# Expert inputs gathered by indirect DMA from normed rows in HBM, instead of by 0/1 products on TensorE

## The chip, the cores and the metric

The kernel runs on one core of a Trainium2 chip. The metric is the device time of one execution in microseconds (us), from runs on the chip; lower is better.

## The reference, cut to what matters

Two blocks are computed in float32 at width 1024. The second has two layers (`DEPTH = 2`) of attention followed by a mixture of experts, and the change lies in the latter. Layer 0 routes 512 tokens (256 latent, 256 context), layer 1 only the 256 latent ones. Each token goes to 2 of 32 experts, each with 512 hidden units:

```python
hf = _modulate(_rmsnorm(x, g_ffn[i]), sh_f, sc_f)      # h * (1 + scale) + shift
...
def _hier_moe(h, ...):          # group by argmax, then top 2 of its 8 experts
    ...
    xb = h_pad[tok_buf].reshape(n_blocks, MOE_BLOCK, d)
    y = (silu(xb @ w_gate[e]) * (xb @ w_up[e])) @ w_down[e]
    out = segment_sum(y * w_buf[:, None], tok_buf)
```

So there are 1024 choices of an expert in layer 0 and 512 in layer 1. Every expert has three matrices of 2 MB, 201 MB for a layer. Latent and context tokens have their own gain (norm weight times 1 + scale) and shift for each of the 1024 features.

## The kernel before, in words

The work is written once, in Python, and laid out for five engines that run side by side and wait on each other by semaphores. TensorE is PE, VectorE is DVE, ScalarE is ACT, GpSimd is POOL, SyncE is SP. A scheduler places the instructions; inside `with self.pinned()` PE keeps the order in which the code has them.

**Before a mixture (`attention`, from L1367).** While the attention's output product runs, `after(m)` transposes each 128 features of the residual into token rows and stores them: one copy (`tok`, L1390), and in layer 0 a second with the rounding rest (`low`, L1394), because these rows are later the operand of products in the fast float32r format. `moe` (L1670) then takes each token's 1/rms, `route` (L1493) picks the experts and gives `pos` (for each token and expert its slot, or 0) and `wt` (its weight and its 1/rms, as a high and a low part).

**A pair of experts.** The 32 experts are done as 16 pairs of 64 + 64 slots (128 columns). For pair p the loop in `moe` has, on PE in this order: `up(...,0)`, the gate product (`pgu`, 32 matmuls); `slots(p)` (`pst`), which turns the 0/1 selection `sel` and reads each slot's weight off; `add` of the pair before for features 0 to 3 (`psy`); `up(...,1)` (again `pgu`); `add` 4 and 5; `hidden` (silu, product, four transposes `phe`); then `gather` for pairs to come, if one is due; `add` 6 and 7; `down` (`pdn`, 32 matmuls). `add` brings the result back to the tokens by a product with the turned selection `selT` and DVE adds it to the residual `xT` (L1906). An expert with more than 64 tokens is finished in `overflow`, a loop with a count read at run time, which stands ahead of the pairs.

**The gather (L1761).** `chosen` compares `pos` with 1 to 64 (`sel`, 0 or 1). `gather` multiplies the token rows by `sel`: for each of the 8 feature blocks `pxe` in PSUM, over two halves of the tokens, in layer 0 over latent and context and over copy and rest. `pin` multiplies a row of rms values by `sel`, ACT makes shift times that row (L1799), DVE adds context's share (L1805) and gain times `pxe` (L1807). So `xe` holds h times rms, and `hidden` multiplies by 1/rms. In layer 0 one `gather` serves two pairs (256 columns); in layer 1 it serves one. The first is taken apart and its pieces lie between the first gate product's matmuls.

**The weights.** `Ahead` streams the expert weights, 192 pieces of 1 MB a layer, over the SP queue, in order, into a ring of buffers. A piece is loaded once its buffer's earlier piece has been used. The ring has 15 buffers in layer 0 (L1955: `h0`, `h1`, four of `base`, `b0`, `b1`, `b4`, `b5`, and five of `more_room`) and 20 in layer 1. Up to 14 (18) of them are filled ahead of the routing.

PSUM has eight banks: four in pool `pm` for the large products, four in `pt` for `pst`, `psy`, `phe`, `pin` and `pxe`. `selT` has a single buffer.

Of the kernel before, what the change touches and what calls it, by code (L numbers as in the profile page):

```python
# [22 lines left out]
BIG = 12582912.0  # L23

# [68 lines left out]
class Net:  # L93
# [7 lines left out]
    def setup(self):  # L101
# [7 lines left out]
        self.mod = self.pool("mod", 1)  # L109
        self.cols = c.tile([P, NCOL], F32, name="cols")  # L110
# [1115 lines left out]
    def attention(self, l, x, xT, norm, mods, ex, wx):  # L1226
# [141 lines left out]
        with self.dense(), self.tc.tile_pool(reuse_waits="tile", name="ao", bufs=1) as sc:  # L1368
            self.table(AF.Abs_reciprocal_sqrt)

            toks = [(("b2", "x"), ("b3", "xc")), (("b2",),)][l]
            toks = [[self.place(n, [P, 2, D], F32R if len(z) == 2 else F32, "tok") for n in z] for z in toks]
# [5 lines left out]
            def after(m):  # L1378
# [7 lines left out]

                at = lambda z: z.rearrange("p t (k m a) -> p t m a k", k=8, m=8)[:, :, m]
                pv = ps.rearrange("p u (a k) -> p u a k", k=8)
                for r in range(nx):
                    nc.scalar.activation(at(toks[r][0]), pv[:, 2 * r:2 * r + 2], AF.Copy)  # L1390
                def low():
                    for r, z in enumerate(toks):
                        if len(z) == 2:
                            nc.vector.tensor_tensor(at(z[1]), pv[:, 2 * r:2 * r + 2], at(z[0]), op=ALU.subtract)  # L1394
                if m < KD - 1:
                    low()
                k0 = {3: 0, 6: 4, 7: 7}.get(m)
                if k0 is None:
                    return low
# [9 lines left out]
                return low  # L1409
# [18 lines left out]
            self.low = after(KD - 1)  # L1428
# [10 lines left out]
    def moe_consts(self):  # L1439
# [8 lines left out]
        self.onesr = self.ones.bitcast(F32R)  # L1448

# [15 lines left out]
    def by_rows(self, l, mods, nx, sc):  # L1465
# [10 lines left out]
        nc.vector.tensor_copy(self.rows, ps)  # L1476

# [15 lines left out]
    def route(self, lg, rs, nt, keep, sc):  # L1493
# [70 lines left out]
    def overflow(self, l, m, pos, wt, rs, more, tot, nt, keep, mw, ex):  # L1564
# [6 lines left out]
        with self.tc.For_i(0, n):  # L1571
            with ExitStack() as st:
# [20 lines left out]
                eq = mw.tile([P, 32], F32, name="eq", tag="selT")  # L1593
# [12 lines left out]
                nc.vector.tensor_copy(wx[:, :, 2:4], bc(rs[:, :, None], [P, nt, 2]))  # L1606
# [17 lines left out]
                xe, steps = self.gather(m, sel, mw)  # L1624
                for f in steps:
                    f()
                g = self.up(xe, w, one, 0)
                selT, ws = self.slots(sel, (wh, wl), one, mw)
                add = self.down(m, self.hidden(g, self.up(xe, w, one, 1), ws, mw), selT, ws, w, one, mw)
# [40 lines left out]
    def moe(self, l, toks, xT, ss, lg, mods, ex, room, then):  # L1670
# [6 lines left out]
        with ExitStack() as st:  # L1677
# [4 lines left out]
            rs = keep.tile([P, nt], F32, name="rs")  # L1682
            std = keep.tile([P, 2, nt], F32R, name="std")
            m = (xT, toks, cols, mgain, std)
            with ExitStack() as s2:
# [8 lines left out]
                nc.gpsimd.tensor_copy(rs, r)  # L1694
                nc.gpsimd.tensor_scalar(st1, st1, 1.0 / D, EPS, op0=ALU.mult, op1=ALU.add)
                nc.gpsimd.tensor_tensor(st1, st1, r, op=ALU.mult)
                nc.gpsimd.tensor_copy(std[:, 0], st1)
                nc.gpsimd.tensor_tensor(std[:, 1], st1, std[:, 0], op=ALU.subtract)
                pos, wt, more, tot = self.route(lg, rs, nt, keep, sc)
# [3 lines left out]
            self.overflow(l, m, pos, wt, rs, more, tot, nt, keep, sc, ex)  # L1703
            ex.load(total - len(ex.tiles))
            groups = [slice(0, 64), slice(64, 128)]

            per = 2 * nx
            sel = self.chosen(pos, 0, per, nt, sc)
            xe, steps = self.gather(m, sel, sc, True)

            def first(k):
                for f in steps[:2] if k == 0 else steps[k + 1:k + 2]:
                    f()
            add = None
            for p in range(16):
                Z = slice(128 * (2 * p % per // 2), 128 * (2 * p % per // 2) + 128)
                new = 2 * (p + 1) % per == 0 and p < 15
                ex.until(2 * p + 1)
                w = lambda a, j, k: ex.take(2 * p + a, j, k)
                xz = [v[:, Z] for v in xe]  # L1720
                with self.pinned():
                    g = self.up(xz, w, groups, 0, None, None if p else first)
                    selT, ws = self.slots(sel[:, :, Z], [z[:, :, p] for z in wt], groups, sc)

                    if add:
                        add([0, 1, 2, 3])
                    u = self.up(xz, w, groups, 1)
                    if new:
                        sel = self.chosen(pos, 2 * (p + 1) // per, per, nt, sc)
                    if add:  # L1730
                        add([4, 5])
                    if new and add:
                        add([6, 7])
                    hT = self.hidden(g, u, ws, sc)
                    if p == 15:
                        self.table(AF.Abs_reciprocal_sqrt)
                    if new:
                        xe, steps = self.gather(m, sel, sc)
                        for f in steps:
                            f()  # L1740
                    elif add:
                        add([6, 7])
                    add = self.down(m, hT, selT, ws, w, groups, sc)
# [17 lines left out]
    def gather(self, m, sel, sc, first=False):  # L1761

        nc = self.nc
        toks, std = m[1], m[4]
        nx = len(toks)
        n = sel.shape[2]
        per = 1 if first else 512 // n

        if n == P:
            xe = sc.tile([P, KD, n], F32, name="xe", tag="xe0")  # L1770
            xe = [xe[:, k] for k in range(KD)]
        else:
            xe = [sc.tile([P, 4, n], F32, name="xe", tag=f"xe{i}") for i in range(2)]
            xe = [xe[k // 4][:, k % 4] for k in range(KD)]
        row = sc.tile([P, nx, n], F32, name="row", tag="row")

        def step(k0):
            got = []
            if k0 == 0:

                ps = self.pt.tile([P, nx, n], F32, name="pin", tag="t")
                for u in range(2 * nx):
                    for i in range(2):
                        self.mm(ps[:, u // 2], bc(std[:, i, u:u + 1], [P, P]), sel[:, u], u % 2 == 0 and i == 0, u % 2 == 1 and i == 1)
                nc.scalar.activation(row, ps, AF.Copy)
            for r in range(nx):
                ps = self.pt.tile([P, per, n], F32, name="pxe", tag="t")
                for j in range(per):
                    K = slice((k0 + j) * P, (k0 + j) * P + P)
                    parts = len(toks[r])  # L1790
                    for i, z in enumerate(toks[r]):
                        for t in range(2):
                            s = sel[:, 2 * r + t]
# [220 lines left out]
def bc(ap, shape):  # L2014
    return ap.to_broadcast(shape)
# [58 lines left out]
```

## Time and profile before

| what | value |
|---|---|
| time, median of 3 runs | 2374.86 us (2373.95 to 2375.71) |
| the profiled execution's own time | 2374.64 us |
| its span, first to last instruction | 2372.9 us |
| granted PE clock, mean over the span | 0.980 |
| PE busy / DVE / ACT / POOL | 94% / 55% / 39% / 6% |
| DMA, mean over the span | 261 GB/s |
| expert weights | 384 pieces of 1 MB |

The span lies 1.74 us below the execution's own time. PE is busy for most of the span, but its matmuls are pipelined, so busy time says little of how near it is to its limit. DMA varies from stage to stage, from 89 GB/s in one fortieth of the span to 420 GB/s in others.

### The profile page before, as it was taken

Reading aid. Unit: us, or ns where it says so; the run is one execution under the profiler, and the core shown is the slowest. Engines: PE = TensorE matmul, PEld = TensorE weight load, DVE = VectorE, ACT = ScalarE, POOL = GpSimd, SP = SyncE. Lnnn points to the kernel's source line nnn. Section 1 sums busy time; section 2 is a strip of 40 time slices with the busy share of each in tenths; the row PEclk is TensorE's granted clock in tenths of the full one; section 3 lists DMA queues with packets and bytes.
Section 4 is the critical chain, followed back from the end, with each engine's and each line's share of the span. In section 5 each row is a group of like instructions: output and inputs, shape, how many; then the busy total and the mean of one; then the engine's idle time right before and its main releaser. Section 6 shows DMA issues by size and latency. Waiting matters only on the chain. (4 is left out here: it accounts for less than half of the span.)

```text
span 2372.9 us, 36247 instructions
## 1 busy us (share of the span) xinstructions
PE 2237.7 (94%) x13798; PEld 1543.6 (65%) x13798; DVE 1309.6 (55%) x3420; ACT 929.6 (39%) x1932; POOL 145.6 (6%) x247
## 2 busy tenths in 40 slices
PE   7999999989999999999799999999898899999998
PEld 6778899778789987777544344444377744444443
DVE  8776666766766665676443444444488523233233
ACT  5655555645555543576311111111256522122122
POOL 2000000110011101200100000000011000000000
PEclk9999999999999999999899999999998999999999
DMA  7364655544665553257389999999643789999996
GB/s 277 110 244 136 224 185 186 196 154 143 216 198 189 180 181 124 89 179 234 107 354 405 373 374 373 374 373 374 241 167 101 269 325 419 419 419 419 420 419 269
DMA packets 178836, 619.29 MB, mean 261 GB/s; under 512 B 9952, under 2 KB 55200, under 8 KB 129504
## 3 DMA queue, kind: packets, MB, share of 16 engines
q1 hardware_dynamic: 177072, 612.54, 68.4%
q0 software_dynamic: 1040, 2.27, 0.4%
q8 instruction: 111, 1.82, 0.3%
q10 hardware_dynamic: 544, 2.10, 0.2%
q14 instruction: 69, 0.57, 0.1%
HBM read 615.81 MB, written 1.05 MB: 260 GB/s over the span
## 5 line engine op out<-in xcount | busy, mean ns | idle before, releaser
L220 DVE TENSOR_TENSOR lo<-w,hi 128x512 fp32r<-128x512 f32 x592 | 424.8, 719 | 256.2 <-ACT hi L219 247.2
L219 ACT ACTIVATE hi<-w 128x512 fp32r<-128x512 f32 x592 | 371.1, 631 | 394.1 <-PE acc L298 157.2
L291 PE MATMUL pgu<-w,xe 128*64 128x512 f32 x2048 | 455.2, 595 | 0.4 <-DVE xe L1807 0.4
L291 PEld LDWEIGHTS pgu<-w,xe 128*64 128x64 f32 x2048 | 143.0, 137 | 276.1 <-issue 270.3
L297 PE MATMUL acc<-lo,hT 128*128 128x512 f32 x624 | 248.3, 398 | 8.7 <-DVE lo L220 8.5
L296 PE MATMUL acc<-hi,hT 128*128 128x512 f32 x624 | 250.2, 403 | 5.6 <-ACT hT L1220 4.5
L298 PE MATMUL acc<-hi,hT 128*128 128x512 f32 x624 | 247.9, 398 | 0.0
L291 PE MATMUL pdn<-w,heT 128*64 128x512 f32 x1024 | 228.5, 599 | 0.9 <-ACT heT L1870 0.9
L335 PE MATMUL gu<-fT,hi 128*128 128x256 f32 x704 | 199.4, 283 | 0.0
L337 PE MATMUL gu<-fT,lo 128*128 128x256 f32 x704 | 199.2, 283 | 0.0
L336 PE MATMUL gu<-fT,hi 128*128 128x256 f32 x704 | 199.2, 283 | 0.0
L1906 DVE SCALAR_TENSOR_TENSOR xT<-psy,mcol,xT 128x256 f32<-128x256 f32 x384 | 159.9, 477 | 12.5 <-PE psy L291 9.3
L291 PEld LDWEIGHTS pdn<-w,heT 128*64 128x64 f32 x1024 | 71.1, 137 | 136.2 <-issue 131.5
L1892 DVE SCALAR_TENSOR_TENSOR y<-pdn,ws,y 128x512 fp32r<-128x512 f32 x64 | 48.0, 750 | 177.9 <-ACT y L1891 177.9
L297 PEld LDWEIGHTS acc<-lo,hT 128*128 128x128 f32 x624 | 119.1, 191 | 34.0 <-DVE lo L220 11.1
L291 PE MATMUL psy<-selT,y 128*128 128x256 f32 (+1 forms) x528 | 119.6, 351 | 21.8 <-DVE xT L1906 19.0
L296 PEld LDWEIGHTS acc<-hi,hT 128*128 128x128 f32 x624 | 118.8, 190 | 32.0 <-ACT hT L1220 5.1
L1891 ACT ACTIVATE y<-pdn,ws 128x512 fp32r<-128x512 f32 x64 | 44.0, 687 | 235.9 <-PE pdn L291 235.9
L336 PEld LDWEIGHTS gu<-fT,hi 128*128 128x128 f32 x704 | 135.1, 192 | 0.7
L335 PEld LDWEIGHTS gu<-fT,hi 128*128 128x128 f32 x704 | 135.1, 192 | 0.7
L337 PEld LDWEIGHTS gu<-fT,lo 128*128 128x128 f32 x704 | 135.1, 192 | 0.0
L298 PEld LDWEIGHTS acc<-hi,hT 128*128 128x128 f32 x624 | 118.6, 190 | 24.7 <-issue 0.8
(517 smaller groups left out, 3311.4 us busy)
## 6 DMA issues: line engine op xcount, KB each, us to landing
w<-in_w_gate SPq DMA_DIRECT2D x128, 1024.0 KB, 11.0
w<-in_w_up SPq DMA_DIRECT2D x128, 1024.0 KB, 12.3
w<-in_w_down SPq DMA_DIRECT2D x128, 1024.0 KB, 12.0
w<-in_w_ada SPq DMA_DIRECT2D x48, 1024.0 KB, 5.2
w<-in_ffn_w_gu SPq DMA_DIRECT2D x44, 1024.0 KB, 5.1
w<-in_ffn_w_down SPq DMA_DIRECT2D x22, 1024.0 KB, 5.0
w<-in_xa_w_kv SPq DMA_DIRECT2D x16, 1024.0 KB, 6.0
w<-in_od_w_in SPq DMA_DIRECT2D x12, 1024.0 KB, 5.2
```

The source lines that it names most:

```text
L219: nc.scalar.activation(hv, src, AF.Copy)
L220: nc.vector.tensor_tensor(lv, src, hv, op=ALU.subtract)
L291: z = self.nc.tensor.matmul(ps, a, b, start=start, stop=stop)
L296: nc.tensor.matmul(ps, ah, wh, start=first, stop=False)
L297: nc.tensor.matmul(ps, ah, wl, start=False, stop=False)
L298: nc.tensor.matmul(ps, al, wh, start=False, stop=last)
L335: nc.tensor.matmul(ps, wh, ah, start=first, stop=False)
L336: nc.tensor.matmul(ps, wh, al, start=False, stop=False)
L337: nc.tensor.matmul(ps, wl, ah, start=False, stop=last)
L1891: nc.scalar.activation(ys[0][:, S], dn[i], AF.Copy, scale=ws[:, 0:1])
L1892: nc.vector.scalar_tensor_tensor(ys[1][:, S], dn[i], ws[:, 0:1], ys[0][:, S], op0=ALU.mult, op1=ALU.subtract)
L1906: nc.vector.scalar_tensor_tensor(xT[b][:, c], ps[:, i, q], cols[:, 40 + c, b:b + 1], xT[b][:, c], op0=ALU.mult, op1=ALU.add)
```

## The change

The token rows are kept once, in plain float32 (in layer 0 with their feature gain already on them, by `gain_rows`). After the norm, ACT multiplies them by 1/rms and they are written to a tensor in HBM. `route` puts each token's number (less 1024) in the place where 1/rms was. For every pair, `slots` reads the number of each slot's token off `pst` and POOL issues an indirect DMA that fetches those rows into `xr`; empty slots have an index out of bounds and fetch nothing. PE turns the rows (`turned`, eight transposes a pair) and ACT (in layer 0 with DVE) adds the shift. In layer 0 a product with ones (`pbk`) tells latent from context slots. `pin`, `row`, the `pxe` products and the factor in `hidden` go. The fetch for pair p + 1 is issued behind pair p's gate product and used behind its `hidden`. `selT` has three buffers, the ring of layer 0 gains `b2`, `b3` and `x` (18 buffers).

```diff
@@ attention
-            toks = [(("b2", "x"), ("b3", "xc")), (("b2",),)][l]
-            toks = [[self.place(n, [P, 2, D], F32R if len(z) == 2 else F32, "tok") for n in z] for z in toks]
+            toks = [self.place(n, [P, 2, D], F32, "tok") for n in ("b2", "b3")[:nx]]
...
+                    if both:
+                        nc.vector.tensor_tensor(toks[r][:, :, M], ps[:, 2 * r:2 * r + 2], bc(grow[:, r, None, M], [P, 2, P]), op=ALU.mult)
+                    else:
+                        nc.scalar.activation(toks[r][:, :, M], ps, AF.Copy)
...
+            grow = self.gain_rows(mods, nx) if both else None
@@
+    def gain_rows(self, mods, nx):
+        nc = self.nc
+        rows = self.place("x", [P, nx, D], F32, "grow")
+        for r in range(nx):
+            for h in range(2):
+                ps = self.pt.tile([P, 512], F32, name="pgr", tag="t")
+                for j in range(4):
+                    nc.tensor.matmul(ps[:, j * P:j * P + P], bc(mods[1][:, 1, 4 * h + j, r:r + 1], [P, P]), self.ident,
+                                     start=True, stop=True)
+                nc.scalar.activation(rows[:, r, 512 * h:512 * h + 512], ps, AF.Copy)
+        return rows
@@ route
+        nc.gpsimd.tensor_copy(w3[:, :, :, 2:4], bc(self.number[:, 0:nt, None, None], [P, nt, 16, 2]))
-        nc.gpsimd.tensor_copy(w3[:, :, :, 2:4], bc(rs[:, :, None, None], [P, nt, 16, 2]))
@@ moe
+                for u in range(nt):
+                    z = toks[u // 2][:, u % 2]
+                    nc.scalar.activation(z, z, AF.Copy, scale=r[:, u:u + 1])
+                    nc.scalar.dma_start(rows[u * P:u * P + P], z)
+                pos, wt, more, tot = self.route(lg, nt, keep, sc)
                 self.table(AF.Silu)
-                self.low()
...
+            xr = self.place("xc", [P, D], F32, "xr") if nx == 2 else sc.tile([P, D], F32, name="xr", tag="xe1")
+            nc.gpsimd.memset(xr, 0.0)
+            def pair(p):
+                sel = self.chosen(pos, p, 2, nt, sc)
+                return self.slots(sel, [z[:, :, p] for z in wt], groups, sc, rows, xr)
+            nxt = pair(0)
+            self.overflow(l, m, pos, wt, more, tot, nt, keep, sc, ex)
             ex.load(total - len(ex.tiles))
+            xe = self.turned(xr, nxt[2], nx, sc)
             add = None
             for p in range(16):
+                selT, ws, _ = nxt
                 ex.until(2 * p + 1)
                 w = lambda a, j, k: ex.take(2 * p + a, j, k)
                 with self.pinned():
+                    g = self.up(xe, w, groups, 0)
+                    if p < 15:
+                        nxt = pair(p + 1)
                     if add:
                         add([0, 1, 2, 3])
+                    u = self.up(xe, w, groups, 1)
                     if add:
                         add([4, 5])
+                    hT = self.hidden(g, u, sc)
                     if p == 15:
                         self.table(AF.Abs_reciprocal_sqrt)
+                    if p < 15:
+                        xe = self.turned(xr, nxt[2], nx, sc)
+                    if add:
                         add([6, 7])
                     add = self.down(m, hT, selT, ws, w, groups, sc)
@@ gather goes (33 lines), instead:
+    def turned(self, xr, blk, nx, sc):
+        nc = self.nc
+        xe = sc.tile([P, KD, P], F32, name="xe", tag="xe0")
+        x8 = xr.rearrange("s (p k) -> s k p", k=KD)
+        for k0 in range(0, KD, 4):
+            ps = self.pt.tile([P, 4, P], F32, name="pxe", tag="t")
+            for j in range(4):
+                z = nc.tensor.transpose(ps[:, j], x8[:, k0 + j], self.ident)
+                if self.pin:
+                    self.tc.keep_in_program_order(z)
+            for j in range(4):
+                k = k0 + j
+                shift, gain = (self.rows[:, i, 0, k:k + 1] for i in range(2))
+                if nx == 1:
+                    nc.scalar.activation(xe[:, k], ps[:, j], AF.Identity, scale=gain, bias=shift)
+                else:
+                    nc.scalar.activation(xe[:, k], ps[:, j], AF.Identity, bias=shift)
+                    nc.vector.scalar_tensor_tensor(xe[:, k], blk, gain, xe[:, k], op0=ALU.mult, op1=ALU.add)
+        return [xe[:, k] for k in range(KD)]
@@ slots
-                selT = sc.tile([P, nt, P], F32R, name="selT", tag="selT")
+                selT = sc.tile([P, nt, P], F32R, name="selT", tag="selT", bufs=3)
...
+        at = sc.tile([P, 1], I32, name="at", tag="at", bufs=2)
+        nc.vector.tensor_scalar(at, w4[0][:, 2:3], float(NONE), None, op0=ALU.add)
+        nc.gpsimd.indirect_dma_start(xr, None, rows, bass.IndirectOffsetOnAxis(ap=at, axis=0), bounds_check=nt * P - 1,
+                                     oob_is_err=False)
+        blk = None
+        if nt == 4:
+            ps = self.pt.tile([P, P], F32, name="pbk", tag="t")
+            for t in range(2):
+                self.mm(ps, self.onesr, sel[:, 2 + t], t == 0, t == 1)
+            blk = sc.tile([P, P], F32, name="blk", tag="blk", bufs=2)
+            nc.scalar.activation(blk, ps, AF.Copy)
@@ run
-        ex = Ahead(self, 0, [self.places[n] for n in ("h0", "h1")] + self.base + [self.places[n] for n in ("b0", "b1", "b4", "b5")])
+        ex = Ahead(self, 0, [self.places[n] for n in ("h0", "h1")] + self.base + [self.places[n] for n in ("b0", "b1", "b4", "b5", "b2", "b3", "x")])
```

## Rows read from the trace of the kernel before

**Rows 1.** Windows: length, busy us by engine, clock, DMA share, GB/s; three stretches.

```profile
1172.00:1707.00 535.00, 502.94 (x2480) 231.57 (x2480) 232.01 (x600) 86.88 (x173) 10.04 (x34) 0.99 0.86 352
...
1902.00:2353.00 451.00, 448.12 (x2428) 215.41 (x2430) 133.35 (x390) 92.14 (x224) 7.72 (x33) 0.99 0.99 407
...
1947.00:2330.00 383.00, 383.00 (x2102) 186.04 (x2104) 117.57 (x343) 79.00 (x194) 5.88 (x26) 1.00 1.01 419
```

**Rows 2.** Timeline of PE, layer 0, the first pair: start us, us, what.

```profile
1173.34 2.07 PE L291 MATMUL pin<-sel,std 128*128 128x256 f32 x8 [6.45 <-issue]
...
1178.35 1.08 PE L291 MATMUL pgu<-w,xe 128*64 128x512 f32 x4 [0.36 <-DVE xe L1807]
...
1193.14 0.68 PE L291 MATMUL pst<-identr,sel 128*128 128x160 f32 x4
```

**Rows 3.** Timeline of PE, layer 0, a gather late in the stage, and the end.

```profile
1633.65 1.16 PE L291 MATMUL pin<-sel,std 128*128 128x256 f32 x8
...
1642.37 7.09 PE L291 MATMUL pdn<-w,heT 128*64 128x512 f32 x32
...
1685.08 0.68 PE L291 MATMUL pst<-identr,sel 128*128 128x160 f32 x4
...
1707.03 1.45 PE L291 MATMUL psy<-selT,y 128*128 128x256 f32 x10
```

**Rows 4.** Timeline of PE, layer 0, a pair without a gather.

```profile
1256.57 0.68 PE L291 MATMUL pst<-identr,sel 128*128 128x160 f32 x4
...
1259.12 1.49 PE L291 MATMUL psy<-selT,y 128*128 128x512 f32 x4 [0.91 <-DVE xT L1906]
...
1269.45 0.72 PE L1866 MATMUL phe<-identr,he 128*128 128x128 f32 x4 [0.70 <-DVE xT L1906]
...
1285.40 0.68 PE L291 MATMUL pst<-identr,sel 128*128 128x160 f32 x4
```

**Rows 5.** Waits, layer 0: engine, line, on whom: us, times, longest.

```profile
ACT selT L1847 <- PE psy L291: 89.5, 14, 12.0
...
PE psy L291 <- DVE xT L1906: 19.0, 22, 1.0
```

**Rows 6.** Timeline of PE, layer 1, one pair.

```profile
2086.40 0.45 PE L291 MATMUL pst<-identr,sel 128*128 128x144 f32 x2
...
2095.83 0.72 PE L1866 MATMUL phe<-identr,he 128*128 128x128 f32 x4
2096.47 0.66 PE L291 MATMUL pin<-sel,std 128*128 128x128 f32 x4
...
2100.68 7.09 PE L291 MATMUL pdn<-w,heT 128*64 128x512 f32 x32
...
2114.57 0.45 PE L291 MATMUL pst<-identr,sel 128*128 128x144 f32 x2
```

**Rows 7.** DMA, 2340 to 2360: GB/s in 40 slices of 0.5 us.

```profile
GB/s 426 442 410 426 393 426 459 393 426 410 426 360 279 279 295 229 262 115 49 57 221 410 303 115 41 0 0 0 0 0 0 0 0 0 0 0 0 0 0 0
```

**Rows 8.** Waits, layer 1: PE's waits for the weights.

```profile
PEld pgu L291 <- DMA w<-in_w_gate: 0.6, 2, 0.3
```

**Rows 9.** DMA: queues (packets, MB, share; 1172 to 1707, 1900 to 2373), issues (count, KB, us to landing).

```profile
q1 hardware_dynamic: 26436, 188.15, 86.0%
...
q1 hardware_dynamic: 25344, 183.51, 94.1%
...
w<-in_w_down SPq DMA_DIRECT2D x60, 1024.0 KB, 19.9
...
wr<-in_w_router POOLq DMA_DIRECT2D x1, 128.0 KB, 8.1
...
xe<-in_g_final POOLq DMA_DIRECT2D x1, 512.0 KB, 3.8
```

**Rows 10.** Instructions by tile and in time: a row-wide ACT pass; DVE behind `pst`.

```profile
L228 ACT ACTIVATE junk<-ctx x1: 1047/1047/1047, 662.7 to 662.7; 128x1024 f32<-128x1024 f32 x1
...
1257.69 0.16 DVE L1852 COPY ws<-w 128x1 f32<-128x1 f32 x1
```

More of the change, by code (lines that the diff above doesn't have):

```diff
@@ L23 @@
 BIG = 12582912.0
+NONE = 1024
 LOOK = 3
@@ L1448, in moe_consts @@
         self.onesr = self.ones.bitcast(F32R)
+        self.number = c.tile([P, 4], F32, name="number")
+        nc.gpsimd.iota(self.number, pattern=[[P, 4]], base=-NONE, channel_multiplier=1, allow_small_or_imprecise_dtypes=True)
         self.same = c.tile([P, 16], F32, name="same")
@@ L1491, in first_max, with route @@
         return m, oh
-    def route(self, lg, rs, nt, keep, sc):
+    def route(self, lg, nt, keep, sc):
         nc = self.nc
@@ L1562, in route, with overflow @@
         return pos, wt, more, tot[0:1, 1:2].bitcast(I32)
-    def overflow(self, l, m, pos, wt, rs, more, tot, nt, keep, mw, ex):
+    def overflow(self, l, m, pos, wt, more, tot, nt, keep, mw, ex):
         nc = self.nc
@@ L1592, in overflow @@
                 nc.vector.tensor_scalar(it, it, 1.0, None, op0=ALU.add)
-                eq = mw.tile([P, 32], F32, name="eq", tag="selT")
+                eq = sc.tile([P, 32], F32, name="eq")
                 nc.vector.tensor_scalar(eq, self.iot[:, 0:32], -1.0, e, op0=ALU.add, op1=ALU.is_equal)
@@ L1623, in overflow @@
                 one = [slice(0, P)]
-                xe, steps = self.gather(m, sel, mw)
-                for f in steps:
-                    f()
+                p, tag = ex.stream.slots[-2]
+                xr = p.tile([P, D], F32, name="xr", tag=tag)
+                nc.vector.memset(xr, 0.0)
+                selT, ws, blk = self.slots(sel, (wh, wl), one, mw, m[1], xr)
+                xe = self.turned(xr, blk, nt // 2, mw)
                 g = self.up(xe, w, one, 0)
-                selT, ws = self.slots(sel, (wh, wl), one, mw)
-                add = self.down(m, self.hidden(g, self.up(xe, w, one, 1), ws, mw), selT, ws, w, one, mw)
+                add = self.down(m, self.hidden(g, self.up(xe, w, one, 1), mw), selT, ws, w, one, mw)
                 for c in range(0, KD, 4):
@@ L1681, in moe @@
             keep = st.enter_context(self.tc.tile_pool(reuse_waits="tile", name="mk", bufs=1))
-            rs = keep.tile([P, nt], F32, name="rs")
-            std = keep.tile([P, 2, nt], F32R, name="std")
-            m = (xT, toks, cols, mgain, std)
+            rows = self.hbm.tile([nt * P, D], F32, name="rows", tag=f"rows{l}")
+            m = (xT, rows, cols)
             with ExitStack() as s2:
@@ L1759, in chosen @@
         return sel
-    def gather(self, m, sel, sc, first=False):
+    def turned(self, xr, blk, nx, sc):
         nc = self.nc
[L1764 to L1793, printed above, removed]
-                            self.mm(ps[:, j], z[:, t, K], s if parts == 2 else s.bitcast(F32), i == 0 and t == 0, i == parts - 1 and t == 1)
-                got.append(ps)
-            for j in range(per):
-                k = k0 + j
-                shift, gain = (self.rows[:, i, :, k] for i in range(2))
-                nc.scalar.activation(xe[k], row[:, 0], AF.Copy, scale=shift[:, 0:1])
-                if nx == 2 and first and k % 2:
-                    b = sc.tile([P, n], F32, name="b", tag="selT")
-                    nc.scalar.activation(b, row[:, 1], AF.Copy, scale=shift[:, 1:2])
-                    nc.gpsimd.tensor_tensor(xe[k], xe[k], b, op=ALU.add)
-                elif nx == 2:
-                    nc.vector.scalar_tensor_tensor(xe[k], row[:, 1], shift[:, 1:2], xe[k], op0=ALU.mult, op1=ALU.add)
-                for r in range(nx):
-                    nc.vector.scalar_tensor_tensor(xe[k], got[r][:, j], gain[:, r:r + 1], xe[k], op0=ALU.mult, op1=ALU.add)
-        return xe, [lambda k0=k0: step(k0) for k0 in range(0, KD, per)]
@@ L1826, in up, with slots @@
         return ps
-    def slots(self, sel, wt, groups, sc):
+    def slots(self, sel, wt, groups, sc, rows, xr):
         nc = self.nc
```

66 lines of the change are left out of this document (15 added, 51 removed).

## The prediction

> **What bounds the kernel now.** I read the windows first, to find the two mixtures and what is full in each; then PE's timeline in each, to price one pair of experts; then the waits, for what ends a wait inside a pair; last the DMA view, for what the weight stream could do if PE were faster.
>
> Layer 0's mixture runs from about 1172 to 1707 us, layer 1's from 1902 to about 2358. In layer 0 PE is busy for 503 of 535 us while DMA has 0.86 of its share at 352 GB/s [rows 1]: PE sets the pace, and the stream has 14% in hand. In layer 1 PE is busy throughout, but so is DMA: 1.01 of its share at 419 GB/s from 1947 to 2330 [rows 1]. There two limits lie on each other. A pair takes PE 2114.57 - 2086.40 = 28.17 us [rows 6], and the stream needs 12 pieces = 12.58 MB / 419 GB/s = 30.0 us for it. PE gains 1.8 us a pair on the stream and lives on the ring's lead of 20 pieces. By the end the lead is gone: the weights arrive until about 2352 [rows 7], a few us before PE ends its last down product, and PE's only waits for weights have begun to show, 0.3 us each [rows 8]. So PE time is worth its full price in layer 0, and next to nothing in layer 1.
>
> **The change in layer 0, on PE.** *Removed.* A gather that serves two pairs holds PE from 1633.65 to 1642.37, 8.72 us [rows 3]; seven such come after the first: 61.0 us. The first costs 1178.35 - 1173.34 = 5.0 us ahead of the first gate product, and its other pieces stretch that product to 1193.14 - 1178.35 = 14.8 us [rows 2], where 32 matmuls take 7.1 [rows 3]: 7.7 more. Together 73.7 us.
>
> *Added in each pair.* Eight transposes: four `phe` of the same shape hold PE for 2096.47 - 2095.83 = 0.64 us [rows 6], so 1.28. Two `pbk` products: four `pst` take 0.68 [rows 4], so 0.34. 1.62 us, 15 times: 24.3.
>
> *A wait that goes.* In a pair without gather PE waits 0.91 us ahead of `psy` and 0.70 ahead of `phe`, for DVE to free a PSUM bank [rows 4]; for `psy` this adds up to 19.0 us [rows 5]. The banks are short because ACT copies `selT` out of `pst` only when the pair before has done its last `psy`: ACT waits 89.5 us in 14 waits, up to 12.0 each [rows 5]. Until then two of the four banks are held. With three buffers of `selT` that copy can start at once. Against it, `pbk` and a second `turned` tile want banks too. Bounds: nothing, and 15 x 1.6 = 24 us; I take 18, nearer the upper end, since the two banks come free ahead of the first `psy` that lacked one.
>
> *The way in.* Now stand in a row: `pst`, the slot number on DVE 1.3 us behind its start [rows 4, 10], the indirect DMA, and 2 us for transposes and first evacuation. No row shows an indirect DMA. From both sides: 3.8 us from issue to landing for 128 rows of 4 KB from the same POOL queue while the stream ran out, 8.1 for 128 KB beside a full stream [rows 9]. The stream is idle here, its ring being full: I take 5, sum 8.3. The DMA page of the Trainium skill ("DMA: Bandwidth & Descriptors", "Anatomy of one DMA") gives about 2.0 us plus bytes over 436 GB/s for a DMA from POOL, an estimate of 2.6 us for 256 KB; the rows do not agree (8.1), and by the page the time would be 2.4 us less and the second rival below out. ACT's four passes over 128x1024, 1.05 us each [rows 10], stand ahead of `route`'s two exponentials: 0 to 4.2 us late, I take 1.5, since DVE's argmax chain covers most. The write of the rows runs beside `route`.
>
> Sum for layer 0: -73.7 + 24.3 - 18 + 8.3 + 1.5 = -57.6 us, which ends it at 1649 instead of 1707.
>
> *The stream's floor there.* 188.15 MB [rows 9] at 419 GB/s take 449 us; 1024 gathered rows of 4 KB are 4.2 MB, 10 us; half a down product follows, 3.5. From 1172 that is 1635, 14 us below my sum. Per pair PE would need 28.83 [rows 4] + 1.62 - 1.2 = 29.25 us, the stream 30.0 + 0.6. The ring, now 18 pieces or 45 us, covers the 1.4 us a pair, but not every time: +5 (0 to 14). Layer 0: -52.6.
>
> **In layer 1.** On PE, 4.21 us of gather [rows 6] give way to 1.28 of transposes: 25.24 a pair, 44 us in 15 pairs. They lie beside the stream and are worth nothing. What is late next is the weights, and the gather adds to their load: 512 rows, 2.1 MB, 5 us. The first gate product is no longer cut up, so buffers come free sooner, -3; the way in is longer by 1. Net +3; both are estimates from the first pair's pieces [rows 2], as no row shows the new way in. Bounds: -6, half of the 13 us that 407 instead of 419 GB/s leave unused over 451 us [rows 1], and +18 (the first rival).
>
> **Ahead of it.** `gain_rows` adds 16 matmuls of a transpose's size, 2.6 us, where PE has gaps; the rest-copies on DVE go: +1.5 (0 to 3).
>
> **Sum.** -52.6 + 3 + 1.5 = -48 us against the profiled execution's own 2374.64 (span 2372.9, and 1.7 around it), which stands 0.2 below the median: **2327 us**.
>
> **The rivals.**
>
> *The fetched rows load a few DMA engines.* Filled slots are the first of each expert's 64, so a pair's 32 rows in layer 1 (64 in layer 0) sit in a few partitions. Each engine moves 419 / 16 = 26 GB/s. If 8 rows of 4 KB fall to each of four engines, these take 1.25 us more a pair, and every piece of weights, spread over all sixteen, waits for them: 20 us in layer 1 instead of 5, and in layer 0, where eight engines would have 1.25 us, 8 more. Then 2327 + 15 + 8 = 2350. For it: layer 1 has no slack. Against it: no row shows how partitions go to engines. By the same page ("The descriptor swizzle") an engine takes four neighbouring partitions and again four 32 further on; as an estimate from it, 16 rows an expert then lie on eight engines, 4 each, and this rival costs 5 us, not 23. No run here shows it yet.
>
> *Slower: the rows come late.* `turned` is due 13.5 us behind `pst` in layer 0 [rows 4], 12.3 without the bank waits; the DMA starts at 1.3, so it has 11 us; in layer 1, 9 [rows 6]. PE keeps its order, so behind a late `turned` stand `psy`, `down` and the next gate product, and the stream behind these. A piece of weights takes 19.9 us to land in layer 1 [rows 9]. If the rows queue like that, each pair waits 9 us in layer 0 (+135) and 11 in layer 1 (36.2 a pair instead of 28.17, +120): near 2570. At 15 us, +60 and +14: 2394. The point from which it decides is 14.2 us, where 15 x 3.2 = 48. Against it: a queue of its own, with 8.1 us beside the full stream [rows 9], and a late PE leaves DMA idle, which speeds the fetch.
>
> *Layer 1 gains too.* If the stream could go faster than 419 GB/s, its 44 us would count: 2280. Against it: DMA at 1.01 for 383 us [rows 1].
>
> **How the numbers follow.** A measurement of this kernel tells 0.2%, about 5 us, from no change. My forecast 0.64, with a range of its own of 2304 (full bank relief, no floor, layer 1 at -6) to 2352 (no relief, route 3 late); loaded engines 0.15; late rows 0.12 (0.01 of it each for a small gain and for no change); layer 1 gains 0.05; several small losses together 0.04 (0.02 of it no change, 0.01 on either side). Faster 0.86, same 0.03, slower 0.11. The range 2304 to 2360 takes in the loaded engines and leaves out layer 1's gain and the late rows.
>
> **What would show it.** Right: `pin` and the long `pxe` gone; in layer 0 `pst` to `pst` near 29 to 30.6 us everywhere, `selT` copied at once; in layer 1 near 30, with PE waiting for `w`, and DMA at 419 GB/s from its first release to its end. The step on the stream is wrong if layer 1's pairs fall below 28; that on banks, if the 0.9 and 0.7 us stay; that on the way in, if the first `pgu` comes more than 12 us behind `pos`. The prediction falls if PE's waits ahead of `turned` end on the fetch, or if DMA's rate drops below 400 GB/s while it is full.

## The result, and the profile after

The kernel after takes 2313.85 us (median of 4 runs, 2312.96 to 2314.41) where the kernel before, run beside it, took 2374.4: a ratio of 0.9744, with a 95% interval of 0.9727 to 0.9761, or 60.6 us less. The profiled execution's span is 2312.0 us. The forecast was 2327, so the time came out 13 us below it, inside the likeliest case's own range.

Layer 0's mixture ends at 1642.56 in place of 1707.03, 64.5 us sooner. Layer 1's ends at 2296.99 in place of 2357.74, 60.8 us sooner: it gives 3.7 back. The same windows as before, taken by stage (columns as in [rows 1]):

```profile
1200.00:1400.00 200.00, 198.46 (x954) 84.23 (x952) 89.84 (x268) 40.34 (x114) 9.84 (x21) 1.00 1.01 422
1400.00:1640.00 240.00, 226.53 (x1030) 100.47 (x1026) 94.94 (x275) 41.94 (x111) 9.38 (x19) 1.00 1.00 417
1860.00:2050.00 190.00, 186.06 (x933) 77.19 (x931) 45.14 (x120) 43.26 (x100) 10.27 (x21) 1.00 1.01 422
2060.00:2290.00 230.00, 207.36 (x952) 86.94 (x950) 48.17 (x126) 42.39 (x95) 10.37 (x20) 1.00 1.00 418
```

DMA is now full in both layers. PE is full at the start of each, and has gaps from the middle on. The timeline of PE, one pair of layer 0, early in the stage:

```profile
1300.74 0.68 PE L294 MATMUL pst<-identr,sel 128*128 128x160 f32 x4
1301.25 0.37 PE L294 MATMUL pbk<-sel,ones 128*128 128x128 f32 x2
1301.46 2.08 PE L294 MATMUL psy<-selT,y 128*128 128x512 f32 x8
1303.47 7.09 PE L294 MATMUL pgu<-w,xe 128*64 128x512 f32 x32
1310.49 1.20 PE L294 MATMUL psy<-selT,y 128*128 128x512 f32 x4
1311.53 0.68 PE L1858 MATMUL phe<-identr,he 128*128 128x128 f32 x4
1312.04 1.05 PE L1778 MATMUL pxe<-identr,xr 128*128 128x128 f32 x8
1312.89 1.19 PE L294 MATMUL psy<-selT,y 128*128 128x512 f32 x4
1314.02 7.09 PE L294 MATMUL pdn<-w,heT 128*64 128x512 f32 x32
...
1327.90 0.68 PE L294 MATMUL pst<-identr,sel 128*128 128x160 f32 x4
```

`pin` and the long `pxe` are gone. The pair takes 27.16 us where the shortest took 28.83 [rows 4], though it holds `pbk` (0.21 us to the next start) and eight transposes (0.85). Both waits of [rows 4] are gone. So it goes up to the ninth pair; then the weights are late. The timeline of PE in layer 0 at that place:

```profile
1429.60 4.72 PE L294 MATMUL pgu<-w,xe 128*64 128x512 f32 x18
1435.62 3.65 PE L294 MATMUL pgu<-w,xe 128*64 128x512 f32 x14 [1.31 <-DMA w<-in_w_gate]
```

And in layer 1, one pair near its end:

```profile
2154.43 0.45 PE L294 MATMUL pst<-identr,sel 128*128 128x144 f32 x2
...
2160.70 3.65 PE L294 MATMUL pgu<-w,xe 128*64 128x512 f32 x14 [0.40 <-DMA w<-in_w_up]
...
2175.69 3.65 PE L294 MATMUL pgu<-w,xe 128*64 128x512 f32 x16 [0.42 <-DMA w<-in_w_gate]
2180.65 3.65 PE L294 MATMUL pgu<-w,xe 128*64 128x512 f32 x14 [1.31 <-DMA w<-in_w_gate]
2184.23 0.45 PE L294 MATMUL pst<-identr,sel 128*128 128x144 f32 x2
```

A gate product stops in its middle until its second pieces have landed. Layer 0's last pairs take 30.36 us (four from 1470.79 to 1592.21), layer 1's 30.30 (six from 2062.78 to 2244.55, after a PE-bound 25.35): the stream's pace in both, where layer 1 needed 28.17 on PE before [rows 6].

The new fetch, in layer 0's way in, first on PE's timeline:

```profile
1175.52 1.14 PE L294 MATMUL pst<-identr,sel 128*128 128x160 f32 x4 [4.14 <-POOL identr L1817]
...
1183.54 1.97 PE L1778 MATMUL pxe<-identr,xr 128*128 128x128 f32 x8 [6.47 <-POOL identr L1817]
1185.50 8.69 PE L294 MATMUL pgu<-w,xe 128*64 128x512 f32 x32
```

The same on POOL's:

```profile
1177.55 1.13 POOL L1835 DMA_INDIRECT xr<-rows,at  x1 [2.08 <-DVE ws L1846]
1183.35 0.20 POOL L1817 CAST identr<-wth 128x16 fp32r<-128x16 f32 x1 [4.68 <-DMA xr<-rows,at]
```

And the fetches of layer 0's pairs in the DMA view (count, median us from issue to landing):

```profile
xr<-rows,at POOLq DMA_INDIRECT x15, 8.4
```

With little else to move it lands 5.8 us after its issue starts (1177.55 to 1183.35); beside the full stream it takes 8.4. The transposes of the next pair come 11.3 us behind `pst` (1300.74 to 1312.04), and the issue about 2 us behind it, so in the pairs it is just hidden.

### The profile page after: what moved, and what is told of

The parts are those of the page before. It is cut to its first block, busy times and chain, and to the rows that moved or that the text cites. A ratio compares the mean times of both kernels' runs of the same rounds, so it can differ in the third digit from the quotient of the medians.

```text
span 2312.0 us, 34547 instructions
## 1 busy us (share of the span) xinstructions
PE 2150.5 (93%) x12966; PEld 1462.6 (63%) x12966; DVE 1231.9 (53%) x3265; ACT 928.2 (40%) x1978; POOL 175.1 (8%) x268
## 5 line engine op out<-in xcount | busy, mean ns | idle before, releaser
L294 PE MATMUL pgu<-w,xe 128*64 128x512 f32 x2048 | 486.1, 600 | 36.2 <-DMA w<-in_w_gate 30.9
L294 PEld LDWEIGHTS pgu<-w,xe 128*64 128x64 f32 x2048 | 156.5, 137 | 336.7 <-issue 253.5
L294 PEld LDWEIGHTS pdn<-w,heT 128*64 128x64 f32 x1024 | 79.2, 137 | 132.8 <-issue 123.0
L1862 ACT ACTIVATE heT<-phe 128x512 f32<-128x512 f32 x32 | 19.2, 599 | 318.3 <-PE phe L1858 318.3
L1826 DVE TENSOR_REDUCE w<-pst 128x4 f32<-128x16 f32 x48 | 8.4, 175 | 224.4 <-PE pst L294 223.4
```

What stands on the lines that cost most here:

```text
L294: z = self.nc.tensor.matmul(ps, a, b, start=start, stop=stop)
L1862: nc.scalar.activation(hT, pt, AF.Copy)
```

## The experiments

**The banks alone.** The first two runs take the `selT` buffers apart from the gather. The kernel before gets a second buffer (its loop needs no third), and the kernel after goes back to the number that waits.

```diff
# e1, the kernel before
-                selT = sc.tile([P, nt, P], F32R, name="selT", tag="selT")
+                selT = sc.tile([P, nt, P], F32R, name="selT", tag="selT", bufs=2)
-        ... self.more_room(room, ex, 5) ...     ex, 14, again)
+        ... self.more_room(room, ex, 4) ...     ex, 13, again)
# e2, the kernel after
-                selT = sc.tile([P, nt, P], F32R, name="selT", tag="selT", bufs=3)
+                selT = sc.tile([P, nt, P], F32R, name="selT", tag="selT", bufs=2)
```

> The kernel before with two buffers of selT in place of one (for the SBUF, layer 0's ring is 14 buffers in place of 15). Theory (the wait of selT's copy, through the PSUM banks, cost layer 0 about 2.7 us a pair, which is what 28.83 + 1.05 - 27.16 leaves over in the kernel after): PE's waits ahead of psy and phe go, and 15 pairs give -40 us; the shorter ring costs nothing, as layer 0's stream has 14% in hand; layer 1 unchanged. 2335 (2330 to 2350). Rival (only the two visible waits of 0.91 and 0.70 us go, as the prediction had it): -18 to -24, 2352 to 2356. Rival (the banks don't matter; the pair is shorter for another reason): within 5 us of 2374.

Measured: 2332.82 us, ratio 0.9821 (0.9804 to 0.9837), 42 us less than before without touching the gather, and in layer 0, with the shorter ring, PE shows next to no wait for weights (its weight loads 2.7 us in all, 0.4 at most). The timeline of PE, a pair without gather:

```profile
1316.67 0.68 PE L291 MATMUL pst<-identr,sel 128*128 128x160 f32 x4
1317.18 2.07 PE L291 MATMUL psy<-selT,y 128*128 128x512 f32 x8
1319.18 7.09 PE L291 MATMUL pgu<-w,xe 128*64 128x512 f32 x32
1326.19 1.20 PE L291 MATMUL psy<-selT,y 128*128 128x512 f32 x4
1327.23 0.73 PE L1866 MATMUL phe<-identr,he 128*128 128x128 f32 x4
...
1342.70 0.68 PE L291 MATMUL pst<-identr,sel 128*128 128x160 f32 x4
```

26.03 us in place of 28.83; a pair with gather takes 34.81 in place of 37.81. The two waits of [rows 4] add up to 1.61 us, but the pair lost 2.8: each wait also stretches the short group behind it (four `psy` take 1.49 us behind a wait and 1.20 without one). From the first gather to the last down product layer 0 takes 488.9 us (1177.25 to 1666.14) in place of 533.7 (1173.34 to 1707.03): 44.8, or 2.8 in each of 16 pairs. It starts 3.9 later than in the kernel before, which no run explains, and layer 1 takes 1 us less; so the whole is 42.

> The kernel after with two buffers of selT in place of three, so that the copy of pair p + 1 waits again for the last psy of pair p - 1. Theory (2.7 us a pair of PE): layer 0's pair takes PE 29.9 us in place of 27.16, which is just under the stream's 30.3, so the lead of the ring is never used: 13 pairs of 29.9 in place of 373 us end layer 0 about +15 us, 2329 (2324 to 2335). Rival (1.2 us a pair, as predicted): 28.4 a pair, the stream's end stays the bound, 2314 to 2318.

Measured: 2349.49, ratio 0.9891 (0.9875 to 0.9908), 35.6 more than the kernel after. The size was expected too small: the pair takes 31.43 us, 4.27 more, since here the transposes want banks as well. PE's waits in layer 0 (on whom: us, times, longest) show both:

```profile
PE psy L294 <- DVE xT L1898: 13.2, 14, 1.1
PE psy L294 <- ACT xe L1787: 10.9, 26, 0.5
PE phe L1858 <- DVE xT L1898: 8.9, 14, 0.6
```

With all of the gather's work gone from PE, this kernel gains only 26 us on the kernel before. And to e1, which has the buffers alone, the whole change adds 19 us (2332.82 to 2313.85).

**The stream as bound of layer 1.** Half of layer 1's bytes, on both kernels.

```diff
-        self.views = [(e, j, i) for p in range(16) for j in range(3) for i in range(2) for e in (2 * p, 2 * p + 1)]
+        self.views = [(e, j, i) for p in range(16) for j in range(3) for i in range(1 + (l == 0)) for e in (2 * p, 2 * p + 1)]
...
+        if self.l:
+            return self.tiles[e, j, 0]
         return self.tiles.pop((e, j, k))
```

> The kernel after with half the expert weights of layer 1: the first half of each matrix is loaded and used for both halves (this leaves out the second halves), with the same work on PE. Theory (layer 1 is bound by the weight stream, and its pair takes PE 25.34 us): all 16 pairs at 25.3 in place of 30.3 from the ninth on, -41 us, 2273 (2267 to 2279), no waits of PE on w_gate there. Rival (PE, or the gather's latency, bounds layer 1 as well): 2305 to 2314.

> The kernel before with half the expert weights of layer 1, as in the run above (the second halves are left out). Theory (there PE was the bound with 28.17 us a pair and the stream reached it only at the end): -3 us, 2371 (2366 to 2375). Then the change would be worth about 98 us where both layers are free of the stream, 37 to 41 more than it gives. Rival (the stream already held the kernel before): -15 us or more.

Measured: 2268.32 (0.9549, 0.9533 to 0.9565) and 2374.10 (0.9996, 0.9986 to 1.0005). In the first, layer 1's pairs stay at 25.34 us to the end and DMA falls to 0.58 of its share. The kernel before does not move. Without the stream's bound in layer 1 the change is worth 2374.1 - 2268.3 = 105.8 us in place of 60.6. The 45 us between them are the PE time that layer 1 saves and the stream hides (44 in the prediction).

**The ring of layer 0.**

```diff
-    ... [self.places[n] for n in ("b0", "b1", "b4", "b5", "b2", "b3", "x")])     ...  ex, 14, again)
+    ... [self.places[n] for n in ("b0", "b1", "b4", "b5")])                      ...  ex, 13, again)
```

> The kernel after with layer 0's ring as before: 15 buffers, without b2, b3 and x (13 of them loaded ahead of the routing). Theory (layer 0 ends on the stream, from about the tenth pair on): three pieces of 1 MB less ahead of the first release, 3 x 2.5 us, +7.5 us, 2321 (2318 to 2324), with the same 27.2 us a pair at the start and 30.3 from an earlier pair on. Rival (PE bounds layer 0 to its end): 2313 to 2316.

Measured: 2320.58 (0.9770, 0.9755 to 0.9784), +6.7. The pairs go to 30 us two pairs sooner (1353.40 to 1382.86 is the first long one). Layer 0 does end on the stream, and a piece loaded ahead is worth 2.2 us.

**The price of a fetch to the stream.** In layer 1: three in place of one, none, and one that is empty.

```diff
# e6, behind the fetch (again: two buffers in b2, in layer 1 alone)
+        for z in again:
+            nc.gpsimd.indirect_dma_start(z, None, rows, bass.IndirectOffsetOnAxis(ap=at, axis=0), bounds_check=nt * P - 1, ...)
# e9
+        if nt == 4:
             nc.gpsimd.indirect_dma_start(xr, ...)
# e10
-        nc.gpsimd.indirect_dma_start(xr, ..., bounds_check=nt * P - 1,
+        nc.gpsimd.indirect_dma_start(xr, ..., bounds_check=nt * P - 1 if nt == 4 else 0,
```

> The kernel after with three fetches a pair in layer 1 in place of one (the two further ones go to a buffer that nobody reads, behind the first in POOL's queue). Theory (a gather costs the stream only its bytes, 32 rows of 4 KB a pair, 0.31 us at 422 GB/s; measured 0.35): 2 x 0.31 to 0.35 us for some 15 pairs, +10 us, 2324 (2320 to 2328), a stream-bound pair of 30.9 to 31.0 us. Rival (the rows fall on a few DMA engines, 1.25 us a pair for each fetch): +35 to +40 us, 32.8 us a pair. Rival (the fetch takes nothing from the stream): 2313 to 2315.

> The kernel after without the fetches of layer 1 (this leaves out layer 1's gathered rows: the transposes turn zeros; layer 0 as it is). Theory (every fetch costs the stream the same 0.69 us that each of the two further ones cost, 31.69 - 30.30 = 1.39 for two): a stream-bound pair of 29.6 us, -11 us, 2303 (2301 to 2305). Rival (the one fetch costs only its bytes, 0.31 to 0.35 us, and a second and third on the same queue cost more): 29.95 a pair, -5.5 us, 2308 (2307 to 2310).

> The kernel after with layer 1's fetches bounded to token 0, so that all slots but two are out of bounds and move next to no bytes (this leaves out the other rows of layer 1), while the 128 slots of each fetch are still worked off. Theory (what a fetch costs beyond its bytes is the handling of its 128 slots, filled or not; q0 shows some 130 packets for a fetch that moves 35 rows): half or more of the cost stays, 0.3 to 0.4 us a pair above the run without fetches, 5 to 6 us. Rival (only the rows' bytes cost): the same time as the run without fetches, within 1.5 us.

| fetches a pair in layer 1 | time, us | stream-bound pair, us (pairs) |
|---|---|---|
| none (e9) | 2300.58 (2297.57 to 2301.93) | 29.71 (five from 2085.70) |
| one, empty (e10) | 2303.48 (2303.03 to 2305.49) | 29.78 (five from 2087.78) |
| one (after) | 2313.85 (2312.96 to 2314.41) | 30.17 (five from 2093.71) |
| three (e6) | 2332.68 (2331.21 to 2334.58) | 31.69 (four from 2074.66) |

In the first three the pair just ahead of these five takes 30.9 to 31.2 us, with and without a fetch, and is left out (the 30.30 above has it in). Pair against pair, the first fetch costs 0.46 us, each further one 0.76, the handling of 128 empty slots 0.07. So the theory of e10 fell: it is the rows, not the slots.

The pairs hold only part of the cost. From the first weights behind the routing to the last to land, the stream of layer 1 takes 438.0 us in e9, 437.7 in e10, 446.9 in the kernel after (1845.9 to 2292.8) and 465.7 in e6, by the packets of the trace. Over 15 fetches that is 0.59 us for the first of a pair, and 0.63 for each further one, where 32 rows of 4 KB at 422 GB/s are 0.31. So the simple count by bytes fell too. The queues' rows of the DMA view (packets, MB, share of 16 engines; 2060 to 2240) show what the packets themselves take, first with the empty fetch (e10):

```profile
q0 software_dynamic: 864, 0.00, 0.3%
```

Then with the full one (the kernel after):

```profile
q1 hardware_dynamic: 10320, 75.13, 99.9%
q0 software_dynamic: 864, 0.72, 1.2%
```

Of 180 us, 1.2% is 2.2 us for six fetches, 0.36 each: about their bytes. The rest shows where the stream runs out. The windows of its last 15 us (columns as in [rows 1]), with no fetch (e9), one (the kernel after) and three (e6):

```profile
2265.00:2280.00 15.00, 13.91 (x63) 6.24 (x62) 3.76 (x9) 2.08 (x3) 0.58 (x1) 1.00 0.96 398
2278.00:2293.00 15.00, 13.93 (x62) 5.88 (x59) 3.26 (x8) 2.08 (x3) 0.57 (x1) 1.00 0.71 292
2298.00:2313.00 15.00, 13.93 (x63) 6.25 (x63) 3.81 (x9) 2.08 (x3) 0.57 (x1) 1.00 0.45 185
```

In all three the last piece of weights was issued before the window begins, so the share falls because some of the 16 engines are done while others still work. In e6 it is 0.46 from 2300 to 2304, about half of them. So the fetched rows lie on some of the engines, and these fall behind. In the pairs this does not show (the mean share stays at 1.01 with none, one and three fetches), which fits engines that always have further weights queued. The rival of the loaded engines was right in kind, and its 1.25 us too high: half of the engines with 4 rows each would need 16 KB at 26 GB/s, an estimate of 0.63. The trace does not name the engine of a packet, so which ones they are stays open. In layer 0, where a fetch brings 64 rows, a stream-bound pair is 0.65 us above e9's 29.71, and 64 rows are 0.62 by bytes; no run leaves out layer 0's fetches.

Of the 13 us between e9 and the kernel after, 6.7 lie in the pairs (first to last `pst`: 381.84 against 388.53 us), 3.8 ahead of them (without a fetch the transposes follow `pst` by 2.94 us, with one by 6.79), and the rest behind them, where the stream runs out.

**The margin of the fetch.** It is issued one product later.

```diff
-                    if p < 15:
-                        nxt = pair(p + 1)
                     if add:
                         add([0, 1, 2, 3])
                     u = self.up(xe, w, groups, 1)
+                    if p < 15:
+                        nxt = pair(p + 1)
```

> The kernel after with the fetch for pair p + 1 issued behind the second gate/up product in place of the first, so that the transposes stand some 3 to 4 us behind pst and not some 11 to 13. Theory (a fetch takes about 8 us to land, hidden now by the slack): PE waits 5 to 6 us a pair for the rows in both layers; layer 0 at 32.5 a pair in place of 27.2 and then 30.3 ends +50 us later, layer 1 at 31 to 32 in place of 30.3 from the ninth pair on and 25.3 before +40: 2400 (2360 to 2430). Rival (beside a late PE the rows land in 4 to 5 us): 2320 to 2345.

Measured: 2537.83 (1.0683, 1.0666 to 1.0699), 224 us slower than after. Layer 0's pair takes 37.5 us, layer 1's 35.0 (fourteen of each add 127 and 102 us). PE's timeline in one pair of layer 0:

```profile
1423.20 0.68 PE L294 MATMUL pst<-identr,sel 128*128 128x160 f32 x4
...
1433.11 1.95 PE L1777 MATMUL pxe<-identr,xr 128*128 128x128 f32 x8 [7.25 <-DMA xr<-rows,at]
1434.71 2.05 PE L294 MATMUL psy<-selT,y 128*128 128x512 f32 x4
1436.69 8.06 PE L294 MATMUL pdn<-w,heT 128*64 128x512 f32 x32
1444.58 1.88 PE L294 MATMUL pgu<-w,xe 128*64 128x512 f32 x8
```

The windows around the wait (columns as in [rows 1], the granted clock third from the end):

```profile
1415.00:1425.00 10.00, 9.94 (x48) 4.16 (x47) 4.59 (x16) 0.79 (x3) 0.41 (x3) 1.00 1.01 424
1426.00:1433.00 7.00, 0.00 (x0) 0.00 (x0) 1.42 (x5) 0.49 (x1) 0.00 (x0) 0.68 1.02 419
1433.00:1437.00 4.00, 3.89 (x14) 3.06 (x16) 2.36 (x9) 2.18 (x8) 0.00 (x0) 0.50 0.72 301
1437.00:1445.00 8.00, 8.00 (x34) 2.44 (x32) 2.15 (x5) 0.86 (x2) 0.00 (x0) 0.89 0.33 101
1445.00:1453.00 8.00, 8.00 (x38) 3.19 (x35) 1.43 (x3) 1.11 (x2) 0.00 (x0) 1.00 1.01 426
```

The wait is 7 to 8 us, not 5 to 6. The clock falls while PE stands idle (0.68 in those 7 us), and behind the wait PE runs at half of it, 0.50, the lower of its levels (1.2 GHz in place of 2.4), until well into `pdn`: from the transposes to the end of `pdn` 11.5 us pass where the kernel after takes 8.9. Wait and clock are 9.8 of the 10.3 us that the pair is longer.

**The late start of layer 0.** The gains by DMA in place of products, then larger rings, then a shorter way in, each on top of the last.

```diff
# e8, gain_rows
-                    nc.tensor.matmul(ps[:, j * P:j * P + P], bc(mods[1][:, 1, 4 * h + j, r:r + 1], [P, P]), self.ident, ...)
-                nc.scalar.activation(rows[:, r, 512 * h:512 * h + 512], ps, AF.Copy)
+            nc.gpsimd.dma_start(self.gains[r].rearrange("(m p) -> p m", p=P), mods[1][:, 1, :, r])
+            nc.gpsimd.dma_start(rows[:, r], self.gains[r].partition_broadcast(P))
# e11, also
-    ... ("b0", "b1", "b4", "b5", "b2", "b3", "x")   ex, 14, again)   ("b0", "b4")         ex, 18, last)
+    ... ("b0", "b1", "b4", "b5", "x", "b2", "b3")   ex, 15, again)   ("b0", "b4", "b2")   ex, 19, last)
# e12, also: for two of layer 0's four row blocks
-                    nc.scalar.activation(z, z, AF.Copy, scale=r[:, u:u + 1])
-                    nc.scalar.dma_start(rows[u * P:u * P + P], z)
+                        nc.gpsimd.tensor_scalar(z, z, r[:, u:u + 1], None, op0=ALU.mult)
+                        nc.gpsimd.dma_start(rows[u * P:u * P + P], z)
# and in layer 1 xr cleared on ACT
```

> The kernel after with gain_rows built by two small DMAs for each of latent and context (gain columns to HBM and back to all partitions) in place of 16 products on PE. Theory (these products, 3.9 us on PE between the last attention product and the output product, are most of the 4.5 us by which layer 0's mixture starts later): -3.5 us, 2310.3 (2309 to 2312). Rival (the late start is from another order of the work earlier, or DVE's product with the gains): 2313 to 2314.5.

> The kernel after with the gains by DMA as in the run before that, x put ahead of b2 and b3 in layer 0's ring and loaded ahead of the routing, and b2 as a 21st buffer of layer 1's ring, 19 of them loaded ahead of the routing. Theory (both layers end on the stream; a piece more ahead of the first release is worth 2.5 us in layer 1, and in layer 0 nothing, as all 18 are loaded by then in either order): 2308.3 - 2.5 = 2306 (2304 to 2308). Rival (the ring is no longer what counts): 2308 to 2310.

> The kernel of the run with the rings, and a shorter way in: in layer 0 two of the four scalings of the token rows and their stores on POOL in place of ACT, so that ACT's exponentials for the weights come some 2 to 3 us sooner; in layer 1 the clearing of xr (0.95 us on POOL, between the two copies that pst waits for) on ACT. Theory (both layers end on the stream, which starts with the first release, so what the way in loses goes to the end): -2.4 in layer 0, -1 in layer 1, 2302.5 (2300 to 2305). Rival (the way in hangs on something else, or POOL's 3 us for a scaling make the rows late): 2305 to 2309.

Measured: 2308.34 (2305.80 to 2310.95; 0.9717, 0.9703 to 0.9730), 2307.51 (2305.47 to 2308.92; 0.9719, 0.9706 to 0.9733) and 2308.09 (2307.00 to 2311.96; 0.9724, 0.9711 to 0.9737). e8 gains 5.5 us on the kernel after, somewhat more than expected, and no run of the three is as slow as one of the kernel after. Its trace shows 3.6 of them as the earlier start of layer 0 (first `pst` at 1171.94 in place of 1175.52). e11's ring shows in the trace as expected (first to last `pst` of layer 1 386.4 us in place of e8's 389.1), but the times of the three can't be told apart. e12's way in failed. In layer 1 it is 0.9 us shorter, as meant. In layer 0 it is 1.2 longer: POOL's scalings slow DVE beside them. The timeline of DVE in e12:

```profile
1159.05 1.62 DVE L1705 SCALAR_TENSOR_TENSOR lg<-lg,rs,sb 128x36 f32<-128x36 f32 x4
...
1162.70 0.48 DVE L1497 TENSOR_TENSOR ao<-ls,am 128x32 f32<-128x32 f32 x1
```

That of POOL in e12:

```profile
1159.12 5.74 POOL L1713 TENSOR_SCALAR tok<-tok,rs 128x1024 f32<-128x1024 f32 x2 [5.00 <-DVE rs L202]
```

And the same two groups of DVE in the kernel after:

```profile
1163.84 0.76 DVE L1708 SCALAR_TENSOR_TENSOR lg<-lg,rs,sb 128x36 f32<-128x36 f32 x4
...
1166.62 0.19 DVE L1500 TENSOR_TENSOR ao<-ls,am 128x32 f32<-128x32 f32 x1
```

0.86 + 0.29 = 1.15 us. And the exponentials, which did come sooner, were not what was late: DVE does the weights behind `pos` in either order. The Trainium skill ("GPSIMD Engine Reference", "1. Specifications") lists POOL's SBUF interface as shared with VectorE, with contention for instructions of two SBUF inputs; the two slowed groups are of that kind, though others of that kind beside them were not slowed.

## Why the prediction was right, and where it was off

| term | predicted | measured | from |
|---|---|---|---|
| gathers that go, layer 0 | -73.7 | -73.7 | no `pin` or long `pxe` left |
| transposes and `pbk`, 15 pairs | +24.3 | +16 | 0.85 + 0.21 a pair |
| bank waits | -18 (0 to -24) | -44.8 | e1, layer 0 |
| way in with ACT's passes | +9.8 | +9.3 | see below |
| stream's floor | +5 (0 to 14) | +24.3 | see below |
| ahead of it (`gain_rows`) | +1.5 (0 to 3) | +4.5 (e8: 5.5) | start of layer 0 |
| layer 1 | +3 | +3.7 | ends of the layers |
| sum | -48 | -60.7 | |

**The gather and the transposes.** Right in kind. Eight transposes take 0.85 us, not twice the 0.64 of the `phe` in [rows 6]; without bank waits four `phe` take 0.51 as well (1311.53 to 1312.04).

**The banks: the step that was mis-sized.** It named the cause (the copy of `selT`, [rows 5]), but bounded it by the two idle times of [rows 4], 1.6 us a pair. e1 shows 2.8: a wait on PE costs more than its idle row, as the group behind it is stretched too. So the pairs were not near 29 to 30.6 us everywhere, as forecast, but 27.16 up to the ninth. The gain is as large as the gather's own net gain in layer 0 (-73.7 + 16 + 9.3 + 4.5 = -44), and has nothing to do with the gather.

**The stream's floor: mis-sized the other way.** 13 pairs at PE's 27.16 would be 353.1 us from 1219.25; the trace has 373.0. From 1592.21 to the end another 50.4 pass, where PE alone needs 45.9 (27.16, and 18.7 for what follows the last gate product, by the rows of the pair at 1300.74): +24.3 together. The same is left of -69 us (-64.5, less the later start of 4.5) when the other terms of layer 0 are taken off. The floor itself, 1635, was right to 3 us: the stage ends at 1642.6 after a start 4.5 us later. Its price was not, as PE's sum was put at 1649; with the measured bank and transpose terms it would have ended at 1614, 21 us ahead of the floor. So the errors of 27 and of 19 us belong together: whatever PE gains past the stream's pace is given back. That the sum still came within 13 us is owed to this, and not to the size of its terms. e5 shows the same floor from the side of the ring.

**The way in.** From `pos` to the first gate product 14.1 us pass (1171.42 to 1185.50) against 11.4 (1166.93 to 1178.35): +7.7 when the 5.0 counted among the gathers is added, and 1.6 for a first gate product of 8.7 us instead of 7.1. That this makes 9.3 where 9.8 was forecast is in part luck. From `pst` to the gate product 9.98 us pass, not 8.3; from `pos` to the first product behind it 4.1 in place of 6.4, where 1.5 more was forecast for ACT's passes; and the 1.6 is a lower clock, which the forecast did not have. By its own sign (more than 12 us behind `pos`) this step would be wrong, but its terms come to 16.2 (11.4 - 5.0 + 8.3 + 1.5): the sign did not fit the sum. PE had stood idle for 4.14 and 6.47 us; the windows of the transposes and of the gate product's start:

```profile
1183.50:1185.50 2.00, 1.96 (x8) 1.57 (x8) 1.23 (x6) 0.80 (x4) 0.28 (x2) 0.50 0.68 156
1185.50:1190.00 4.50, 4.50 (x15) 1.43 (x16) 1.79 (x7) 1.37 (x6) 0.00 (x0) 0.64 0.95 393
```

The eight transposes take 1.97 us there, and 1.05 in the pair at 1300.74, where the clock is 1.00. The fetch took 5.8 us where 5 were taken. By the Trainium skill ("DMA: Bandwidth & Descriptors", "Anatomy of one DMA") it would have been 2.6, as an estimate; the trace does not agree, neither here nor beside the stream (8.4).

**`gain_rows`.** Not in gaps of PE: 28 of its 32 rows stand in one group of 3.39 us at 1099.10, between the last attention product and the output product. As layer 0 ends on the stream, which starts with the first release, a late start goes to the end whole.

**Layer 1.** Right, and for the reason given: e3 and e4 show PE's 45 us under the stream. Inside the +3.7 the fetch was priced too low: it costs the stream 8.9 us, not 5. So what the forecast put at -2 besides must be near -5, and no run takes it apart.

**The rivals.** Loaded engines: right in kind, with 0.6 us a fetch and not 1.25; some engines are done some 10 us ahead of the others. By the Trainium skill ("DMA: Bandwidth & Descriptors", "The descriptor swizzle") the rows lie on more engines than that rival assumed, and its cost there was 5 us, as an estimate; the trace agrees, with 8.9 us where the bytes alone are 4.7. Late rows: not in the kernel after, whose waits on the fetch are 0.3 us in layer 1, but e7, with the margin gone, measured 2538, near the 2570 of that rival's dearer case. It came there by another road: the rows land in 8.3 us, as in the kernel after, and not in 20, but they are asked for too late. Layer 1 gains too: refuted, DMA gives 422 GB/s with and without the fetch.

## What to carry to other kernels

Where a second resource stands close behind the bound, a sum over the first one alone can be wrong in every term and still come out near: work out the time at which the second ends, and price only what lies above it. A small buffer that holds a PSUM bank can cost as much as a change of the work saves, so try its second copy by itself first. Where transfers queue, a load on some of its engines hides in the mean rate until the queue runs out: look there as well. A fetch's latency is hidden only while it is issued a landing time ahead of its use (here 8 us, and 2 for its index); one product later each pair lost 10.3 us, a quarter of it to the lower clock behind the wait.

## What was not expected of the hardware

- Idle times of PE of 0.9 and 0.7 us cost 2.8 us a pair (e1), and one of 7 us cost 2.6 more through the lower clock behind it (e7).
- An indirect fetch of 128 slots takes POOL 1.0 us to issue, lands 5.8 us after the issue starts with little else to move and 8.4 beside a full stream, and with 32 rows costs that stream 0.59 us, twice its bytes' time, because some engines fall behind, while empty slots take next to nothing (e9, e10).
- The stream holds 422 GB/s on one core, 1.01 of the DMA share, where [rows 1] showed 419.
- Two POOL passes over 128x1024 of 2.9 us slowed some of DVE's short operations beside them from 0.19 to 0.40 and 0.48 us (e12).
